# Stick-breaking attention: the diagonal chunks of row blocks 2 and 6 turned by transfers, and the keys copied in place by ScalarE

## The chip, the cores and the metric

The kernel runs on one core of one Trainium2 chip. The metric is the device time of one execution in microseconds (us).

A core has five engines that each follow a queue of their own, in order: PE (TensorE, matrix products; its weight loads are shown apart as PEld), ACT (ScalarE), DVE (VectorE), POOL (GpSimd) and SP (SyncE, which here issues nearly all transfers, DMAs). They meet by semaphores. PE writes to PSUM, an accumulator memory; tiles live in SBUF, 128 partitions wide.

## The reference

A trunk of two layers over 1024 tokens of width 1024: layer 0 has a gated recurrence, layer 1 stick-breaking attention, and each a SwiGLU block behind it. Only the attention is touched by the change. It has 16 heads of width 64:

```python
for blk in range(seq // Q_BLOCK):            # Q_BLOCK = 128
    t0 = blk * Q_BLOCK; t1 = t0 + Q_BLOCK
    z = jnp.einsum("bhqd,bhkd->bhqk", q[:, :, t0:t1], k[:, :, :t1]).astype(jnp.float32) * scale
    strict = s_idx < t_idx                   # causal, the diagonal left out
    log_fail = jnp.where(strict, jax.nn.log_sigmoid(-z), 0.0)
    suffix = lax.cumsum(log_fail, axis=3, reverse=True) - log_fail
    weights = jnp.where(strict, jnp.exp(jax.nn.log_sigmoid(z) + suffix), 0.0)
    outs.append(jnp.einsum("bhqk,bhkd->bhqd", weights.astype(vb.dtype), vb))
```

## The kernel before

**Precision.** Factors are kept as a high and a low part, and products are made from the parts: three matmuls for each product of the dense layers (`mm3`, lines 143 to 145). In attention, a head's queries, 64 wide, stand on one half of the partitions and their low parts on the other half (`Q[q][hx]`). The keys (`KK[q][hx]`, 128 partitions by 2 by 1024) hold the high part in row 0 and the low part in row 1, the same on both halves. So two matmuls over all 128 partitions (`z_part`, L1680 and L1681) give the product of queries and keys.

**Chunks.** For a head, the rows are 8 blocks j of 128 queries. Each block has a diagonal chunk (its keys in the last 512 begun, 128 to 512 wide), and blocks 4 to 7 also a full chunk of 512 keys: 12 chunks a head. A chunk goes through `z_part` (PE), `z_rest` (ACT, a sigmoid, L1693) and `scan` (DVE, a running product from right to left, L1700 and L1703), which leaves the tile `w`.

**Turning.** The products with the values need `w` with keys on the partitions, as two fp16 parts. This is done in two ways:
- `turn_weights`: ACT copies the high part, DVE subtracts the low part (`wx`, L1713 and L1714), and a transposing transfer, issued by SP, writes the turned blocks (`wt` L1721 for full chunks, `wd` L1717 for diagonal ones). Before the change this way is taken by the full chunks and the diagonal chunks of blocks 3 and 7 (`by_transfer`). The four `wx` buffers go round.
- `t_part` and `t_split`: PE turns blocks of 128 by 128 (`wt_ps`, L1732), ACT rounds them to fp16 (`th`, L1741), DVE subtracts (`tl`, L1742). This way is taken by the diagonal chunks of blocks 0, 1, 2 and 4, 5, 6.

`av_part` (L1760) then adds up the products with the values over a *unit*, a block of 128 keys against 512 queries. There are 12 units a head: 4 for the first half of the queries and 8 for the second.

**Order.** Heads come in 8 pairs q, with hx 0 or 1. The queues of PE, ACT, DVE, POOL and SP in attention are written out by hand, in a loop over the 192 units. Each step takes one chunk (10 steps ahead of its unit, 13 ahead near the end), the turning of the chunk before, a unit's products, and 2 parts of the projection of the next pair's queries, keys and values (`qkv_steps`, PE tile `qk_ps`). A pair is thus 24 steps. When the projections run out, at step 161 of 192, the loop has only `out_fill`, parts of the output projection (`ob`); their inputs come back from DRAM by transfers (`back`, L1883).

**Keys.** When a half of a pair's keys is projected, `evacuate` lets DVE scale it into `two`, ACT round the high part (L1663) and DVE subtract the low part (L1645). A step later `spread` has SP issue four transfers (L1642), each of a head's two rows, to the upper and to the lower half of `KK`.

`later` and `soon` are lists of small tasks that the loop takes up one step at a time; a task of `soon` comes at the start of a step.

Of the kernel before, what the change touches and what calls it, by code (L numbers as in the profile page):

```python
# [8 lines left out]
F32 = mybir.dt.float32  # L9
F32R = mybir.dt.float32r  # L10
BF16 = mybir.dt.bfloat16
F16 = mybir.dt.float16
# [5 lines left out]
P = 128  # L18
# [4 lines left out]
NB = 512  # L23
# [11 lines left out]
def trunk(  # L35
# [21 lines left out]
    nc = tc.nc  # L57
    f32 = lambda t: t.bitcast(F32)
# [336 lines left out]
    with ExitStack() as st:  # L395
# [17 lines left out]
        two = lp.tile([P, ND], I32, name="two")  # L413
# [28 lines left out]
        wide = lambda tag, bufs, dt=F32: lp.tile([P, S], dt, tag=tag, name=tag, bufs=bufs)  # L442
# [1045 lines left out]
    with ExitStack() as st:  # L1488
        ap = st.enter_context(tc.tile_pool(name="ap", bufs=1))
# [5 lines left out]
        psQ = qs.enter_context(tc.tile_pool(name="psQ", bufs=2, space=PSUM, side="right", reuse_waits="tile"))  # L1495


        unit = ap.tile([P, NB], F32, name="unit")
        nc.gpsimd.memset(unit[:, 0 : NB - P], 0.0)
        nc.gpsimd.tensor_scalar_mul(unit[:, NB - P :], ident, UP)  # L1500
        g2 = ap.tile([P, ND], BF16, name="g2")
# [2 lines left out]
        Q, KK, VV, VT = {}, {}, {}, {}  # L1504
        top, bot = slice(0, HD), slice(HD, P)
# [14 lines left out]
        def stage(task, steps=1):  # L1520
            soon.append([steps, task])
# [76 lines left out]
        def evacuate(q, which, n, ps):  # L1598
            full = lambda tag, m: [ap.tile([P, m, S], F32R, tag=tag, name=tag, bufs=4 if m == 1 else 3) for _ in range(2)]
            cs = slice(n * NB, (n + 1) * NB)  # L1600
            if which == 2:
                if n == 0:
                    VT[q] = ap.tile([P, S + 1], F32, tag="vt", name="vt", bufs=2)
                    nc.gpsimd.memset(VT[q][:, 0:1], 0.0)
                    VV[q] = ap.tile([P, 2, NT, 2, HD], F16, tag="v", name="v", bufs=2)
                t = ap.tile([P, NB], F32, tag="t", name="t", bufs=1)
                after = VT[q][:, n * NB + 1 : (n + 1) * NB + 1]
                nc.vector.scalar_tensor_tensor(after, ps, f32(sv[q]), rbc[n], op0=ALU.mult, op1=ALU.mult)
                yield
                if q == NP - 1:  # L1610
                    some = [(p, n) for p in range(NP - 2)]
                    bring_back(*some[:3], *([(NP - 2, 0)] * n), *some[3:])
                nc.vector.tensor_sub(t, VT[q][:, cs], after)
                vx = ap.tile([P, 4, 2, P], F16, tag="vx", name="vx", bufs=2)
                t3 = t.rearrange("p (b c) -> p b c", b=4)

                def low():
                    nc.vector.scalar_tensor_tensor(
                        vx[:, :, 1], t3, 1 / UP, vx[:, :, 0], op0=ALU.mult, op1=ALU.subtract
                    )  # L1620
                    for hx, a in enumerate((top, bot)):
                        nc.sync.dma_start(
                            VV[q][:, hx, 4 * n : 4 * n + 4].rearrange("p b h c -> p (b h) c"),
                            vx[a].rearrange("p b h c -> p (b h c)"),
                            transpose=True,
                        )
                def high():
                    nc.scalar.activation(vx[:, :, 0], t3, AF.Copy, scale=1 / UP)
                    stage(low)

                stage(high, 2)
                return
            two = ap.tile([P, 2, NB], F32R, tag="two", name="two", bufs=2)

            def spread():
                for hx, (a, b) in enumerate(((top, bot), (bot, top))):
                    if which == 0:
                        nc.sync.dma_start(f32(Q[q][hx])[a, cs], f32(two)[a, 0])
                        nc.sync.dma_start(f32(Q[q][hx])[b, cs], f32(two)[a, 1])
                    else:  # L1640
                        for half_ in (top, bot):
                            nc.sync.dma_start(f32(KK[q][hx])[half_, :, cs], f32(two)[a])  # L1642

            def low():
                nc.vector.tensor_sub(two[:, 1], t, f32(two)[:, 0])  # L1645
                stage(spread)

            if which == 0:
                t = ps
                if n == 0:  # L1650
                    Q[q] = [x[:, 0] for x in full("q", 1)]
                nc.scalar.copy(two[:, 0], t)
                yield
                low()
            else:
                t = f32(two)[:, 1]
                nc.vector.tensor_mul(t, ps, rbc[n])
                if n == 0:
                    KK[q] = full("kk", 2)
                yield  # L1660

                def high():
                    nc.scalar.copy(two[:, 0], t)  # L1663
                    stage(low)

                stage(high)
# [20 lines left out]

        def z_rest(ps, q, hx, j, ci, c0, c1, diag):
            n = min(c1, (j + 1) * P) - c0
            tag = f"w{j}" if diag and j != 3 else "w"  # L1690
            F = ap.tile([P, n], F32, tag=tag, name=tag, bufs=1 if tag != "w" else 3)
            W[q, hx, j, ci] = F
            nc.scalar.activation(F, ps[:, 0:n], AF.Sigmoid, scale=rs[:, j : j + 1])  # L1693

        def scan(q, hx, j, ci, c0, c1, diag):
            F = W[q, hx, j, ci]
            n = min(c1, (j + 1) * P) - c0
            rev = F[:, ::-1]
            if diag:
# [5 lines left out]
        T = {}  # L1705

        def by_transfer(q, hx, j, ci, c0, c1, diag):
            return not diag or j % 4 == 3

        def turn_weights(q, hx, j, ci, c0, c1, diag):  # L1710
            F = W[q, hx, j, ci].rearrange("p (b c) -> p b c", c=P)
            wx = ap.tile([P, 4, 2, P], F16, tag="wx", name="wx", bufs=4)
            nc.scalar.copy(wx[:, :, 0], F)  # L1713
            nc.vector.tensor_sub(wx[:, :, 1], F, wx[:, :, 0])  # L1714
            if diag:
                T[q, hx, j] = ap.tile([P, 8, P], F16, tag="wd", name="wd", bufs=2)
                nc.sync.dma_start(T[q, hx, j], wx.rearrange("p b h c -> p (b h c)"), transpose=True)  # L1717
                return
            if j == 4:
                T[q, hx] = ap.tile([P, 8, 4, P], F16, tag="wt", name="wt", bufs=2)  # L1720
            nc.sync.dma_start(T[q, hx][:, :, j % 4], wx.rearrange("p b h c -> p (b h c)"), transpose=True)  # L1721

        def unit_list(q, hx):
            kbs = ((0, 1, 2, 3), (4, 5, 6, 7, 0, 1, 2, 3))
# [2 lines left out]
        def t_part(q, hx, G, kb, first, last):  # L1727
            j0 = max(kb, 4 * G)
            tp = psT.tile([P, NB], F32, tag="T", name="wt_ps")
            for j in range(j0, 4 * G + 3):  # L1730
                c = (j - 4 * G) * P
                nc.tensor.transpose(  # L1732
                    tp[:, c : c + P], W[q, hx, j, kb // 4][:, (kb % 4) * P : (kb % 4 + 1) * P], ident
                )
            return tp

        def t_split(tp, q, hx, G, kb, first, last):
            q0 = (max(kb, 4 * G) - 4 * G) * P
            th = ap.tile([P, NB - P], F16, tag="th", name="th", bufs=3)
            tl = ap.tile([P, NB - P], F16, tag="tl", name="tl", bufs=3)  # L1740
            nc.scalar.copy(th[:, q0:], tp[:, q0 : NB - P])  # L1741
            nc.vector.tensor_sub(tl[:, q0:], tp[:, q0 : NB - P], th[:, q0:])  # L1742
            return th, tl

        av, oo = {}, {}
# [1 line left out]
        def av_part(tht, q, hx, G, kb, first, last):  # L1747
            q0 = (max(kb, 4 * G) - 4 * G) * P
            if first:
                av[0] = psO.tile([P, NB], F32, tag="o", name="av_ps")  # L1750
            ps = av[0]
            if kb // 4 != G:
                turned = [T[q, hx][:, 2 * kb + x].rearrange("p j c -> p (j c)") for x in range(2)]
                parts_ = [(0, NB, t, 0) for t in turned]
            else:
                parts_ = [(NB - P, NB, T[q, hx, 4 * G + 3][:, 2 * (kb % 4) + x], 0) for x in range(2)]
                if tht is not None:
                    parts_ = [(q0, NB - P, t, q0) for t in tht] + parts_
            for i, (c0, c1, t, t0) in enumerate(parts_):
                nc.tensor.matmul(  # L1760
                    ps[:, c0:c1], lhsT=VV[q][:, hx, kb], rhs=t[:, t0 : t0 + c1 - c0],
# [4 lines left out]
            a, b = (top, bot)[:: 1 if hx == 0 else -1]  # L1766
# [38 lines left out]
        units = [u for q, hx in heads for u in unit_list(q, hx)]  # L1805
# [28 lines left out]
        with tc.manual_schedule(engines={E.PE, E.Activation, E.DVE, E.Pool, E.SP}):  # L1834
# [33 lines left out]
            c = 0  # L1868
# [5 lines left out]
            for u in range(-LEAD, len(units)):  # L1874
# [9 lines left out]
                for a in some:  # L1884
                    z_rest(z_part(*a), *a)
                    if u % 2 or u < -2:
                        scan(*a)
# [3 lines left out]
                if u % 2 == 0 and u >= 0:  # L1891
                    av_part(ready.pop(u, None), *units[u])
                if u % 2 == 0 and 0 <= u + 2 < len(units):
                    two = {x: t_part(*units[x]) for x in (u + 2, u + 3) if x % 12 < 8 and x % 4 < 3}
                    for x, tp in two.items():
                        ready[x] = t_split(tp, *units[x])
                if u % 2 == 0 and u >= -2:
# [70 lines left out]
```

## Time and profile before

| | |
|---|---|
| time before, median of 3 runs | 2144.06 us (2139.91 to 2144.3) |
| profiled execution | 2142.03 us |
| its span | 2140.0 us |
| granted TensorE clock, mean | 0.997 |
| busy share of the span | PE 99%, DVE 83%, ACT 53%, POOL 6% |
| attention | about 985 to 1420 us of the span |

The profile is of one execution. Its own time is 2.03 us above its span. Busy times are of whole instructions as the profiler has them; matmuls overlap, so a matmul's duration is longer than the time from its start to the next one's start. L numbers are lines of the kernel.

### The profile page before, as it was taken

How to read it: one execution, taken by the hardware profiler on the slowest of the kernel's cores; microseconds unless marked ns; L12 is line 12 of the kernel's file. 1: busy time of each engine (PE TensorE's matmuls, PEld its weight loads, DVE VectorE, ACT ScalarE, POOL GpSimd, SP SyncE). 2: the span in 40 equal slices, each digit the busy share in tenths (PEclk: the TensorE clock that was granted, in tenths of full speed). 3: DMA queues.
4: the chain of work that ended last, by engine and by line, in shares of the span. 5: the costliest groups of instructions: out<-in, count | busy, mean ns of one | idle time of the engine just before them, and what ended most of it. 6: DMA issues, size and time to landing. Idle time of an engine off the chain costs nothing.

```text
span 2140.0 us, 28244 instructions
## 1 busy us (share of the span) xinstructions
PE 2116.5 (99%) x10222; PEld 1735.1 (81%) x10222; DVE 1778.7 (83%) x2609; ACT 1137.5 (53%) x1838; POOL 125.8 (6%) x100
## 2 busy tenths in 40 slices
PE   8999999999999999999999999899999999999998
PEld 7888888888888888888777777678888888888887
DVE  7887768888888888896899999867888888888886
ACT  6567435444443545565666666544544344454556
POOL 1222020000000000000000000002000000000002
PEclk9999999999999999999999999999999999999999
DMA  7111421334445875536888888983234544587442
GB/s 237 50 50 40 153 98 58 117 113 157 138 148 162 276 241 148 160 121 143 160 177 178 176 177 177 230 257 99 64 104 128 162 135 151 193 274 229 130 153 89
DMA packets 424109, 323.87 MB, mean 151 GB/s; under 512 B 135065, under 2 KB 330785, under 8 KB 423969
## 3 DMA queue, kind: packets, MB, share of 16 engines
q1 hardware_dynamic: 423808, 321.80, 53.1%
q8 instruction: 80, 1.31, 0.3%
q14 instruction: 61, 0.49, 0.1%
q10 hardware_dynamic: 160, 0.27, 0.0%
HBM read 184.09 MB, written 83.36 MB: 125 GB/s over the span
## 4 chain that ended last, share of the span: by engine, by line
PE 96%; DVE 2%; DMA 1%; ACT 1%; issue 1%; SPq 0%; DVEq 0%; ACTq 0%
PE p_ps L143 18%; PE p_ps L145 18%; PE p_ps L144 18%; PE qk_ps L143 4%; PE qk_ps L145 4%; PE qk_ps L144 4%; PE av_ps L1760 3%; PE a_ps L144 3%; PE a_ps L145 3%; PE a_ps L143 3%; PE ob_ps L145 3%; PE ob_ps L143 3%; PE ob_ps L144 3%; PE z_ps L1680 2%; PE z_ps L1681 2%; PE i_ps L145 1%
## 5 line engine op out<-in xcount | busy, mean ns | idle before, releaser
L143 PE MATMUL p_ps<-vh,wbh 128*128 128x512 f32 x524 | 204.9, 391 | 0.0
L144 PE MATMUL p_ps<-vl,wbh 128*128 128x512 f32 x524 | 204.5, 390 | 0.0
L145 PE MATMUL p_ps<-vh,wbl 128*128 128x512 f32 x524 | 204.0, 389 | 0.2 <-DVE wbl L726 0.2
L143 PE MATMUL p_ps<-vh,wch 128*128 128x512 f32 x524 | 204.1, 390 | 0.0
L145 PE MATMUL p_ps<-vh,wcl 128*128 128x512 f32 x524 | 204.1, 389 | 0.0
L144 PE MATMUL p_ps<-vl,wch 128*128 128x512 f32 x524 | 203.9, 389 | 0.0
L722 ACT CAST wbh<-sb 128x1024 fp32r<-128x1024 f32 (+2 forms) x69 | 69.6, 1009 | 192.6 <-DVE sb L702 192.6
L1693 ACT ACTIVATE w<-z_ps,rs 128x128 f32<-128x128 f32 (+1 forms) x192 | 110.9, 580 | 94.0 <-PE z_ps L1681 93.5
L145 PE MATMUL p_ps<-vh,wal 128*128 128x512 f32 x396 | 154.0, 389 | 0.0
L143 PE MATMUL p_ps<-vh,wah 128*128 128x512 f32 x396 | 154.0, 389 | 0.0
L144 PE MATMUL p_ps<-vl,wah 128*128 128x512 f32 x396 | 154.0, 389 | 0.0
L145 PEld LDWEIGHTS p_ps<-vh,wbl 128*128 128x128 f32 x524 | 98.4, 188 | 21.6 <-DVE wbl L726 0.7
L145 PEld LDWEIGHTS p_ps<-vh,wcl 128*128 128x128 f32 x524 | 98.3, 188 | 21.0 <-DVE wcl L736 0.6
L144 PEld LDWEIGHTS p_ps<-vl,wch 128*128 128x128 f32 x524 | 98.4, 188 | 20.4
L143 PEld LDWEIGHTS p_ps<-vh,wch 128*128 128x128 f32 x524 | 98.3, 188 | 20.5 <-ACT tb L1181 0.2
L1700 DVE TENSOR_TENSOR_SCAN w<-w,unit 128x128 f32<-128x128 f32 (+3 forms) x128 | 105.0, 831 | 11.7 <-ACT w L1693 11.6
L143 PEld LDWEIGHTS p_ps<-vh,wbh 128*128 128x128 f32 x524 | 98.6, 188 | 19.8 <-ACT U L1181 0.4
L144 PEld LDWEIGHTS p_ps<-vl,wbh 128*128 128x128 f32 x524 | 98.6, 188 | 18.5
L143 PE MATMUL qk_ps<-vh,whi 128*128 128x512 f32 x264 | 111.9, 424 | 0.0
L145 PE MATMUL qk_ps<-vh,wlo 128*128 128x512 f32 x264 | 103.7, 393 | 0.0
L144 PE MATMUL qk_ps<-vl,whi 128*128 128x512 f32 x264 | 103.2, 391 | 0.0
L143 PE MATMUL p_ps<-vh,wd 128*128 128x512 f32 x254 | 99.4, 391 | 0.0
(403 smaller groups left out, 5794.2 us busy)
## 6 DMA issues: line engine op xcount, KB each, us to landing
raw<-in_ffn_w_in SPq DMA_DIRECT2D x88, 512.0 KB, 4.2
vl<-pd SPq DMA_DIRECT2D x128, 256.0 KB, 3.5
pd<-U SPq DMA_DIRECT2D x90, 256.0 KB, 2.3
kk<-two SPq DMA_DIRECT2D x64, 256.0 KB, 4.5
raw<-in_ffn_w_out SPq DMA_DIRECT2D x56, 256.0 KB, 3.7
raw<-in_attn_w_qkv SPq DMA_DIRECT2D x24, 512.0 KB, 5.9
h<-hd SPq DMA_DIRECT2D x32, 256.0 KB, 5.8
hd<-h SPq DMA_DIRECT2D x32, 256.0 KB, 2.0
```

Of the source, the lines that this page charges most:

```text
L143: nc.tensor.matmul(ps, lhsT=wh, rhs=mh, start=first, stop=False, **kw)
L144: nc.tensor.matmul(ps, lhsT=wh, rhs=ml, start=False, stop=False, **kw)
L145: nc.tensor.matmul(ps, lhsT=wl, rhs=mh, start=False, stop=last, **kw)
L722: nc.scalar.copy(self.full(self.wb), self.full(self.sb))
L1680: nc.tensor.matmul(ps[:, 0 : c1 - c0], lhsT=lhsT, rhs=KK[q][hx][:, 0, c0:c1], start=True, stop=False)
L1681: nc.tensor.matmul(ps[:, 0 : c1 - c0], lhsT=lhsT, rhs=KK[q][hx][:, 1, c0:c1], start=False, stop=True)
L1693: nc.scalar.activation(F, ps[:, 0:n], AF.Sigmoid, scale=rs[:, j : j + 1])
L1700: nc.vector.tensor_tensor_scan(rev, rev, unit[:, NB - n :][:, ::-1], 0.0, op0=ALU.mult, op1=ALU.add)
L1760: nc.tensor.matmul(ps[:, c0:c1], lhsT=VV[q][:, hx, kb], rhs=t[:, t0 : t0 + c1 - c0], start=first and i == 0, stop=last and i == len(parts_ ...
```

## The change

Five edits go together.

- Blocks 2 and 6 join those whose diagonal chunk is turned by a transfer (384 wide, so three blocks of high and three of low parts). `wd` holds two row blocks side by side. PE turns only blocks 0, 1, 4 and 5, and `th` and `tl` are 256 wide at most. The products of a unit with the turned diagonal are 256 wide where both row blocks count.
- Keys: a head's half of the partitions gets high and low parts by ScalarE copies within the partitions (four of 64x512 for each half of a pair's keys). Only the high part goes to the other half by a transfer (two of 64x512 for each half of the keys), which is issued one step earlier than before. Beside the low part stand zeros, so the product of the two low parts is left out.
- GpSimd writes these zeros, two of 64x1024 a pair.
- The tile `w` of block 2 comes from the shared three buffers.
- `unit`, the second operand of the diagonal scans, is BF16 instead of F32.

```diff
-        unit = ap.tile([P, NB], F32, name="unit")
+        unit = ap.tile([P, NB], BF16, name="unit")
...
+            sides = ((0, top, bot), (1, bot, top))
+
+            def place(x):
+                for hx, a, b in sides:
+                    if x == 0:
+                        nc.sync.dma_start(f32(KK[q][hx])[b, 0, cs], f32(two)[a, 0])
+                    nc.scalar.copy(KK[q][hx][a, x, cs], f32(two)[a, x])
+
             def spread():
-                for hx, (a, b) in enumerate(((top, bot), (bot, top))):
-                    if which == 0:
-                        nc.sync.dma_start(f32(Q[q][hx])[a, cs], f32(two)[a, 0])
-                        nc.sync.dma_start(f32(Q[q][hx])[b, cs], f32(two)[a, 1])
-                    else:
-                        for half_ in (top, bot):
-                            nc.sync.dma_start(f32(KK[q][hx])[half_, :, cs], f32(two)[a])
+                if which == 1:
+                    place(1)
+                    return
...
             def low():
                 nc.vector.tensor_sub(two[:, 1], t, f32(two)[:, 0])
+                if which == 1:
+                    place(0)
                 stage(spread)
...
                 if n == 0:
                     KK[q] = full("kk", 2)
+                    for hx, a, b in sides:
+                        nc.gpsimd.memset(f32(KK[q][hx])[b, 1], 0.0)
...
-            tag = f"w{j}" if diag and j != 3 else "w"
+            tag = f"w{j}" if diag and j not in (2, 3) else "w"
...
         def by_transfer(q, hx, j, ci, c0, c1, diag):
-            return not diag or j % 4 == 3
+            return not diag or j % 4 >= 2
...
-            for j in range(j0, 4 * G + 3):
+            for j in range(j0, 4 * G + 2):
...
-            nc.scalar.copy(th[:, q0:], tp[:, q0 : NB - P])
-            nc.vector.tensor_sub(tl[:, q0:], tp[:, q0 : NB - P], th[:, q0:])
+            nc.scalar.copy(th[:, q0:], tp[:, q0 : 2 * P])
+            nc.vector.tensor_sub(tl[:, q0:], tp[:, q0 : 2 * P], th[:, q0:])
...
-                parts_ = [(NB - P, NB, T[q, hx, 4 * G + 3][:, 2 * (kb % 4) + x], 0) for x in range(2)]
+                c0 = max(q0, 2 * P)
+                parts_ = [(c0, NB, t, c0 - 2 * P) for t in turned]
...
-                    two = {x: t_part(*units[x]) for x in (u + 2, u + 3) if x % 12 < 8 and x % 4 < 3}
+                    two = {x: t_part(*units[x]) for x in (u + 2, u + 3) if x % 12 < 8 and x % 4 < 2}
```

**PE, at a step that turns blocks for two units.** Before:

```order
L1760 MATMUL av_ps<-wd,v 128x128
L1732 MATMUL wt_ps<-ident,w_8264 128x128
L1732 MATMUL wt_ps<-ident,w_8286 128x128
L1732 MATMUL wt_ps<-ident,w_8303 128x128
L1732 MATMUL wt_ps<-ident,w_8286 128x128
L1732 MATMUL wt_ps<-ident,w_8303 128x128
L143 MATMUL qk_ps<-vh_3_2540,whi 128x512
```

Of the change, at the same step:

```order
L1774 LDWEIGHTS v
L1774 MATMUL av_ps<-wd,v 128x256
L1743 MATMUL wt_ps<-ident,w_8275 128x128
L1743 MATMUL wt_ps<-ident,w_8296 128x128 x2
L143 MATMUL qk_ps<-vh_3_2540,whi 128x512
```

Five turned blocks become three, and the products with the transferred weights are 256 wide. At the next even step one turned block becomes none.

**ACT, where the second half of a pair's keys is placed.** The copies for the keys (`kk`) stand ahead of the sigmoids (`w<-z_ps`) of two steps that follow each other. Before:

```order
L1693 ACTIVATE w<-z_ps,rs 128x512
L1741 CAST th<-wt_ps 128x384
L1741 CAST th<-wt_ps 128x256
L1713 CAST wx<-w_9221 128x4x128
L1693 ACTIVATE w<-z_ps,rs 128x512
L1713 CAST wx<-w 128x4x128
L1558 CAST whi<-raw 128x512
L1693 ACTIVATE w<-z_ps,rs 128x512
L1741 CAST th<-wt_ps 128x128
L1713 CAST wx<-w 128x4x128
L1772 COPY oo<-av_ps 64x512
```

Of the change, at the same steps:

```order
L1704 ACTIVATE w<-z_ps,rs 128x512
L1752 CAST th<-wt_ps 128x256
L1752 CAST th<-wt_ps 128x128
L1725 CAST wx<-w_9205 128x4x128
L1641 CAST kk<-two 64x512 x2
L1704 ACTIVATE w<-z_ps,rs 128x512
L1725 CAST wx<-w 128x4x128
L1558 CAST whi<-raw 128x512
L1641 CAST kk<-two 64x512 x2
L1704 ACTIVATE w<-z_ps,rs 128x512
L1725 CAST wx<-w 128x4x128
L1786 COPY oo<-av_ps 64x512
```

Two copies come ahead of each of two sigmoids; the `th` copies are narrower, and one is gone.

**SP, where the projections run out and the transfers back from DRAM (`odh`, `odl`) begin.** Before:

```order
L1642 DMA kk<-two 64x2x512 x4
L1721 DMA_TRANSPOSE wt<-wx 128x8x128 x2
L1883 DMA vh_3_2532<-odh_0_7885 128x512
L1721 DMA_TRANSPOSE wt<-wx 128x8x128
L1883 DMA vl_3_2533<-odl_0_7886 128x512
L1622 DMA_TRANSPOSE v<-vx 128x8x64 x2
L1883 DMA xg_6477<-odh_0_7887 128x512
L1883 DMA xg_6478<-odl_0_7888 128x512
L1883 DMA vh_3_2540<-odh_0_7889 128x512
L1883 DMA vl_3_2541<-odl_0_7890 128x512
L1883 DMA xg_7655<-odh_0_7891 128x512
L1717 DMA_TRANSPOSE wd<-wx 128x8x128
```

Of the change, the same stretch from the second transfer back on, cut at the same `wd`:

```order
L1732 DMA_TRANSPOSE wt<-wx 128x8x128
L1897 DMA vl_3_2533<-odl_0_7886 128x512
L116 DMA raw<-in_attn_w_o 128x8x128
L1622 DMA_TRANSPOSE v<-vx 128x8x64 x2
L1897 DMA xg_6477<-odh_0_7887 128x512
L1897 DMA xg_6478<-odl_0_7888 128x512
L1897 DMA vh_3_2540<-odh_0_7889 128x512
L1732 DMA_TRANSPOSE wd<-wx 128x6x128
L1897 DMA vl_3_2541<-odl_0_7890 128x512
L1897 DMA xg_7655<-odh_0_7891 128x512
L1732 DMA_TRANSPOSE wd<-wx 128x8x128
```

A transposing transfer for block 2 has come in, and a load of output weights (512 KB) that stood some 35 rows further on now stands ahead of the values' transfers.

More of the change, by code (lines that the diff above doesn't have):

```diff
@@ L1633, in evacuate @@
             two = ap.tile([P, 2, NB], F32R, tag="two", name="two", bufs=2)
-            def spread():
-                for hx, (a, b) in enumerate(((top, bot), (bot, top))):
-                    if which == 0:
-                        nc.sync.dma_start(f32(Q[q][hx])[a, cs], f32(two)[a, 0])
-                        nc.sync.dma_start(f32(Q[q][hx])[b, cs], f32(two)[a, 1])
-                    else:
-                        for half_ in (top, bot):
-                            nc.sync.dma_start(f32(KK[q][hx])[half_, :, cs], f32(two)[a])
+            sides = ((0, top, bot), (1, bot, top))
[4 more added lines that the diff above has]
+                    nc.scalar.copy(KK[q][hx][a, x, cs], f32(two)[a, x])
+            def spread():
+                if which == 1:
+                    place(1)
+                    return
+                for hx, a, b in sides:
+                    nc.sync.dma_start(f32(Q[q][hx])[a, cs], f32(two)[a, 0])
+                    nc.sync.dma_start(f32(Q[q][hx])[b, cs], f32(two)[a, 1])
             def low():
                 nc.vector.tensor_sub(two[:, 1], t, f32(two)[:, 0])
+                if which == 1:
+                    place(0)
                 stage(spread)
@@ L1659, in evacuate @@
                     KK[q] = full("kk", 2)
+                    for hx, a, b in sides:
+                        nc.gpsimd.memset(f32(KK[q][hx])[b, 1], 0.0)
                 yield
@@ L1707, in by_transfer @@
         def by_transfer(q, hx, j, ci, c0, c1, diag):
-            return not diag or j % 4 == 3
+            return not diag or j % 4 >= 2
         def turn_weights(q, hx, j, ci, c0, c1, diag):
             F = W[q, hx, j, ci].rearrange("p (b c) -> p b c", c=P)
+            m = F.shape[1]
             wx = ap.tile([P, 4, 2, P], F16, tag="wx", name="wx", bufs=4)
[L1713 to L1721, printed above, removed]
+            nc.scalar.copy(wx[:, 0:m, 0], F)
+            nc.vector.tensor_sub(wx[:, 0:m, 1], F, wx[:, 0:m, 0])
+            g = (q, hx, j // 4, diag)
+            if g not in T:
+                wide, tag = (2, "wd") if diag else (4, "wt")
+                T[g] = ap.tile([P, 8, wide, P], F16, tag=tag, name=tag, bufs=2)
+            dst = T[g][:, 0 : 2 * m, j % 4 - (2 if diag else 0)]
+            nc.sync.dma_start(dst, wx[:, 0:m].rearrange("p b h c -> p (b h c)"), transpose=True)
         def unit_list(q, hx):
@@ L1738, in t_split @@
             q0 = (max(kb, 4 * G) - 4 * G) * P
[L1739 to L1742, printed above, removed]
+            th = ap.tile([P, 2 * P], F16, tag="th", name="th", bufs=3)
+            tl = ap.tile([P, 2 * P], F16, tag="tl", name="tl", bufs=3)
+            nc.scalar.copy(th[:, q0:], tp[:, q0 : 2 * P])
+            nc.vector.tensor_sub(tl[:, q0:], tp[:, q0 : 2 * P], th[:, q0:])
             return th, tl
@@ L1751, in av_part @@
             ps = av[0]
+            turned = [
+                T[q, hx, G, kb // 4 == G][:, 2 * (kb % 4) + x].rearrange("p j c -> p (j c)") for x in range(2)
+            ]
             if kb // 4 != G:
-                turned = [T[q, hx][:, 2 * kb + x].rearrange("p j c -> p (j c)") for x in range(2)]
                 parts_ = [(0, NB, t, 0) for t in turned]
             else:
-                parts_ = [(NB - P, NB, T[q, hx, 4 * G + 3][:, 2 * (kb % 4) + x], 0) for x in range(2)]
+                c0 = max(q0, 2 * P)
+                parts_ = [(c0, NB, t, c0 - 2 * P) for t in turned]
                 if tht is not None:
-                    parts_ = [(q0, NB - P, t, q0) for t in tht] + parts_
+                    parts_ = [(q0, 2 * P, t, q0) for t in tht] + parts_
             for i, (c0, c1, t, t0) in enumerate(parts_):
```

## Prediction

> **What bounds the kernel now.** I read the page first, for the busy shares.
>
> ```profile
> PE 2116.5 (99%) x10222; PEld 1735.1 (81%) x10222; DVE 1778.7 (83%) x2609; ACT 1137.5 (53%) x1838; POOL 125.8 (6%) x100
> ```
>
> The span is PE's, but a share is a mean over stages. So next come the busy times by stretch, cut at the start of PE's turned blocks, which makes each stretch one head. Columns: stretch, length, then busy time (and instructions) of PE, PEld, DVE, ACT and POOL, the granted clock, the DMA share, GB/s.
>
> ```profile
> 1108.79:1135.47 26.68, 26.68 (x146) 20.33 (x145) 24.24 (x35) 17.70 (x35) 1.09 (x1) 1.00 0.84 185
> 1135.47:1162.45 26.98, 26.98 (x155) 20.62 (x153) 25.38 (x40) 17.55 (x35) 2.80 (x4) 1.00 0.93 170
> ...
> 1350.11:1376.00 25.89, 22.99 (x123) 16.74 (x121) 24.42 (x39) 16.61 (x33) 1.71 (x3) 0.88 0.98 202
> ```
>
> PE fills two heads (a pair, 53.66 us) without a gap. DVE has 49.62 of these 53.66 us, so 4.04 us of room. From about 1366 us, where the projections end, PE has gaps. PE's waits between 985 and 1425 us, as total, times, longest, show where:
>
> ```profile
> PE ob L143 <- DMA vh<-odh: 4.2, 3, 1.7
> PE z_ps L1680 <- ACT w L1693: 2.5, 3, 1.9
> PE ob L144 <- DMA vl<-odl: 1.4, 3, 1.0
> ```
>
> All three belong to the end, waits for what comes back from DRAM and for sigmoids. So there are two stages: 14 heads bound by PE, and an end of some 50 us that is not. Windows of 10 us of the end:
>
> ```profile
> 1360.00:1370.00 10.00, 8.06 (x49) 6.15 (x47) 9.94 (x17) 5.36 (x12) 0.00 (x0) 1.00 1.09 204
> 1370.00:1380.00 10.00, 7.97 (x21) 4.57 (x21) 9.42 (x13) 5.47 (x9) 0.00 (x0) 0.66 0.95 216
> 1380.00:1390.00 10.00, 7.09 (x37) 4.55 (x37) 7.14 (x12) 5.24 (x12) 0.00 (x0) 1.00 1.14 302
> 1390.00:1400.00 10.00, 7.35 (x47) 4.58 (x44) 9.01 (x14) 6.67 (x14) 0.00 (x0) 0.86 1.08 284
> ```
>
> Here the DMA engines are full, and DVE has 35.5 of 40 us: those two share the bound.
>
> **PE's part.** What PE's instructions cost in flow is read from the chain of waits, which merges neighbours (start, length, count):
>
> ```profile
> 1140.43 0.45 PE av_ps L1760 x4
> ...
> 1144.23 0.34 PE av_ps L1760 x4
> ...
> 1144.86 0.24 PE av_ps L1760 x4
> 1145.10 0.55 PE wt_ps L1732 x5
> ```
>
> A turned block costs 0.55/5 = 0.11 us. A group of four blocks of queries had 3 + 2 + 1 turned blocks and now has 2 + 1: 0.33 us less, 0.66 us a head. The products: the three av rows are units of columns 2 x (384 + 128), 2 x (256 + 128) and 2 x (128 + 128). They are now 2 x (256 + 256), 2 x (128 + 256) and 2 x 256: the same columns, in fewer pieces in the third. At 0.45 us for 1024 columns this is nothing. So 14 heads x 0.66 = **9.2 us less** on the bounding engine; 1.3 us more in the last two heads, which I count at nothing since PE waits there anyway (bound: 1.3 gained).
>
> **What takes PE's place: DVE and ACT.** The groups by shape between 1000 and 1400 us (busy us, mean ns | idle before):
>
> ```profile
> L1714 DVE TENSOR_TENSOR wx<-w,wx 128x512 f16<-128x512 f32 x90 | 64.4, 716 | 7.3 <-ACT wx L1713 6.4
> L1713 ACT CAST wx<-w 128x512 f16<-128x512 f32 x91 | 56.7, 624 | 30.1 <-DVE w L1700 12.9 <-DVE w L1703 9.1 <-DMA wd<-wx 2.9
> L1700 DVE TENSOR_TENSOR_SCAN w<-w,unit 128x512 f32<-128x512 f32 x31 | 39.8, 1284 | 7.2 <-ACT w L1693 7.2
> ...
> L1772 ACT COPY oo<-av_ps 64x512 f32<-64x512 f32 x29 | 16.9, 582 | 0.7
> L1742 DVE TENSOR_TENSOR tl<-wt_ps,th 128x384 f16<-128x384 f32 x30 | 16.5, 551 | 14.2 <-ACT th L1741 14.2
> L1741 ACT CAST th<-wt_ps 128x384 f16<-128x384 f32 x30 | 14.4, 480 | 3.9 <-PE wt_ps L1732 2.6
> ...
> L1742 DVE TENSOR_TENSOR tl<-wt_ps,th 128x256 f16<-128x256 f32 x30 | 12.4, 412 | 0.0
> ...
> L1645 DVE TENSOR_TENSOR two<-two 128x512 fp32r<-128x512 f32 x14 | 9.5, 680 | 0.0
> ```
>
> Widths 384, 256, 128 become 256, 128, none: what goes is one 384 wide, 0.551 us on DVE and 0.480 on ACT a group. What comes is one `wx` pair 384 wide. At three quarters of the 512 rows this is 0.54 on DVE and 0.47 on ACT. The sum is zero on both. It moves, though, from the steps where DVE is fullest (full chunks, scans of 512) to those of the diagonal.
>
> The keys' ScalarE copies are new: 8 a pair, at the 0.582 us of the only 64x512 copy (L1772, out of PSUM), 4.7 us a pair. ACT has 35.2 of 53.66 us, so there is room, but they stand ahead of sigmoids for which DVE waits. The tightest place, the second half of a pair's keys:
>
> ```profile
> 1139.19 0.68 DVE L1645 TENSOR_TENSOR two<-two 128x512 fp32r<-128x512 f32 x1
> ...
> 1140.47 0.69 ACT L1693 ACTIVATE w<-z_ps,rs 128x512 f32<-128x512 f32 x1 [0.21 <-PE z_ps L1681]
> 1141.20 0.63 ACT L1713 CAST wx<-w 128x512 f16<-128x512 f32 x1
> 1141.86 0.69 DVE L1714 TENSOR_TENSOR wx<-w,wx 128x512 f16<-128x512 f32 x1
> ...
> 1147.89 0.88 DVE L1742 TENSOR_TENSOR tl<-wt_ps,th 128x384 f16<-128x384 f32 x2
> 1149.01 0.34 PE L1760 MATMUL av_ps<-th,v 128*128 128x384 f16 x1
> ```
>
> The first `tl` is done at 1147.89 + 0.55 = 1148.44. PE wants it for its second product, half of a 0.34 us pair after 1149.01, at 1149.18: 0.74 us of slack. PE will come 2 + 1 + 2 turned blocks earlier, 0.55 us. The low parts' copies wait for DVE's subtraction, done at 1139.87, and two last 1.16, to 1141.03. The sigmoid then ends at 1141.7 instead of 1141.16, the `wx` copy at 1142.3 instead of 1141.83, and DVE's subtraction comes 0.5 us late; the whole queue of DVE shifts, as it is full there. The narrower `tl` gives back 0.14 (551 to 412). So 0.74 - 0.55 - 0.5 + 0.14 = -0.17: PE waits 0.17 us in each of the 7 pairs whose keys are placed inside the loop, **1.2 us back**. Bounds: nothing (ACT is ahead), and the pair's whole gain, 1.3 us, 9 us in all.
>
> In the other head of a pair no keys are placed; by the same sum the slack stays over 0.2 us.
>
> `unit` in BF16: no row shows a scan with it. A subtraction with an fp16 side lasts 716 against 680 ns (L1714, L1645), so the bounds are none and 5% of 1.28 us a scan, either way; DVE has the room, so I take nothing.
>
> **POOL's zeros.** Rows of POOL: start, length.
>
> ```profile
> 965.32 0.42 POOL L1499 MEMSET unit<- 128x384 f32 x1 [642.58 <-DVE rbc L1383]
> ...
> 1153.34 1.09 POOL L1777 TENSOR_TENSOR oo<-oo,vt 128x512 f32<-128x512 f32 x1 [12.12 <-DVE oo L1773]
> 1171.24 2.12 POOL L1777 TENSOR_TENSOR oo<-oo,vt 128x512 f32<-128x512 f32 x1 [16.82 <-DVE oo L1773]
> ```
>
> Scaled by width, a memset of 1024 lasts 0.42 x 1024/384 = 1.1 us, 2.2 a pair, queued ahead of POOL's small factors only, with POOL idle for 12 us and more at a time. The same addition lasts 1.09 or 2.12 us, so POOL and DVE do hold each other up. I take nothing; the bound is that DVE stands still for all 2.2 us. The Trainium skill (SBUF — State Buffer, "Who interferes with whom") says that a VectorE instruction with two SBUF inputs contends with a GpSimd one that reads SBUF, not with one that only writes: by it the zeros cost DVE nothing, and no row here shows a large memset beside such an instruction.
>
> **Transfers.** Rows of SP's issues and one of landing (us at the end):
>
> ```profile
> 1030.87 1.27 SPq L1717 DMA_TRANSPOSE wd<-wx  x1
> ...
> 1035.68 3.41 SPq L1642 DMA_DIRECT2D kk<-two  x4
> ...
> 1047.33 0.58 SPq L116 DMA_DIRECT2D raw<-in_attn_w_qkv  x1
> ...
> 1055.49 0.51 SPq L1638 DMA_DIRECT2D q<-two  x1
> ...
> wd<-wx SPq DMA_TRANSPOSE x30, 3.6
> ```
>
> A pair loses 8 transfers of 256 KB and gains 4 of 128 KB and 4 transposing ones of 192 KB. SP: -6.8 + 4 x 0.55 + 4 x 1.27 = +0.5 us. Bytes: -0.75 MB; a turned byte costs the engines more than a copied one, so I call the load equal. The new transposing transfers are issued a step after their chunk and needed 7 steps later (a step is 53.66/24 = 2.24 us, so 15.7 us), against 3.6 us to landing: hidden. The Trainium skill (VectorE: DVE Perf Modes, "The three transpose paths") speaks against this edit: 1309 ns for a 128x128 block by a transfer against 390 on TensorE. By it, as an estimate, a 384 wide transfer of both parts takes 6 x 1.31 = 7.9 us; the row, 3.6 us for eight blocks, is far below, and decides.
>
> At the end SP and the DMA engines are full. There SP loses one set of keys (3.41 to about 1.1), and gains four transposing issues (4 x 1.27) and, ahead of the values, a weight load of 0.58 that stood later: +3.4 us. As DVE has the other half of this bound, I take a third, **1.2 us**. Bounds: -1.3 (PE's blocks count after all), and 3.4 + 1.7 (the load's 512 KB at 302 GB/s) = 5.1.
>
> **The sum.** -9.2 + 1.2 + 1.2 = -6.8 us. The profiled execution took 2142.03 (span 2140.0 and 2.03 around it), which makes 2135.2; from the median of 2144.06 it is 2137.3. I take 2136. A measurement of this kernel can tell some 0.2% (4.3 us) from no change.
>
> **Rivals.**
> 1. *ACT and DVE become the bound, slower.* Place: the steps where keys are placed. If DVE keeps all its idle time (4.04 us a pair, waits on ACT) and half of the 4.7 us of key copies falls in front of its scans, a pair lasts 53.66 + 2.3 us, and 7 pairs 16 us more: 2158. It decides from 2.7 us of DVE idle time a pair (4.04 less PE's 1.3). For it: DVE at 94% in one head, L1713's 30 us of idle time ahead. Against: ACT's 66%, and that the waits on ACT come where DVE has caught up. 0.15.
> 2. *The gain is eaten at the handoff*: DVE just keeps up with the old pace, 0 in place of -9.2, and the end's 1.2: 2143. POOL holding DVE for 2.2 us a pair would come to this too. 0.17.
> 3. *The end takes it back*: -9.2 + 1.2 + 5.1 = -2.9, 2139, within 0.2%. For it the DMA shares over 1, against it DVE's 9.9 and 9.4. 0.10.
> 4. *The change doesn't do what it says.* The order of instructions shows the narrower turning and half as many key transfers, so I give it nothing.
>
> Forecast: 0.55. Something slower that I don't see: 0.03.
>
> **Range and chances.** The forecast's best is 9.2 + 1.3 + 1.3 below the profiled time, 2130. Above, rivals 2 and 3 reach 2143, the median's side 2145, and DVE's part of rival 1 in small 2149. The range 2130 to 2149 leaves out most of rival 1 and the unseen. Faster by over 0.2% is the forecast, less 0.03 of it that ends close: 0.52. Within 0.2%: 0.03 + 0.17 + 0.10 = 0.30. Slower: 0.18.
>
> **What would show it.** Right: a pair of 52.5 us with PE full, DVE near 49.6 in it, and PE's wait for `tl` of some 0.2 us a pair; the end from the last projection to the last product 1 us longer. Wrong: a pair at 53.66 or more, with PE waiting for `tl` or for sigmoids (rivals 1 and 2), DVE rows stretched beside memsets (the zeros), or waits of `ob` for `vh` and `vl` well over 6 us (rival 3).

## The result, and the profile after

| | before | after |
|---|---|---|
| median of 8 runs each | 2143.78 us (2139.91 to 2144.72) | 2137.22 us (2135.17 to 2138.37) |
| profiled execution | 2142.03 | 2137.39 |
| its span | 2140.0 | 2135.6 |

The ratio is 0.9972, with a 95% interval of 0.9963 to 0.9981: 6.6 us faster by the medians. The forecast was 2136, so 1.2 us from it.

The page's busy times of after, in the order of those of before:

```profile
PE 2106.9 (99%) x10062; PEld 1725.7 (81%) x10062; DVE 1776.9 (83%) x2609; ACT 1173.4 (55%) x1902; POOL 142.6 (7%) x116
```

PE has 160 instructions and 9.6 us of busy time less, ACT 36 us more, and DVE is where it was. The windows of after, cut as before: two heads of one pair, then 10 us pieces of the end (length, busy time of PE, PEld, DVE, ACT, POOL, granted clock, DMA share, GB/s).

```profile
1107.18:1133.07 25.89, 25.89 (x136) 19.70 (x135) 24.76 (x37) 20.19 (x39) 4.03 (x3) 1.00 0.95 199
1133.07:1159.51 26.44, 26.33 (x144) 19.96 (x143) 24.58 (x39) 19.65 (x39) 2.73 (x4) 1.00 0.69 135
...
1360.00:1370.00 10.00, 6.73 (x24) 3.88 (x24) 9.94 (x16) 5.98 (x12) 0.00 (x0) 0.86 1.16 272
1370.00:1380.00 10.00, 5.87 (x22) 3.63 (x23) 6.03 (x9) 3.32 (x8) 0.00 (x0) 0.84 1.07 228
1380.00:1390.00 10.00, 9.15 (x41) 5.99 (x39) 7.54 (x12) 4.73 (x11) 0.00 (x0) 0.62 1.08 266
```

The pair is 25.89 + 26.44 = 52.33 us, against 53.66: the heads are still PE's. PE's waits from 985 to 1425 us (total, times, longest):

```profile
PE z_ps L1691 <- ACT w L1704: 6.4, 6, 2.5
PE ob L143 <- DMA vh<-odh: 4.1, 1, 4.1
PE av_ps L1774 <- DVE oo L1787: 0.9, 1, 0.9
PE ob L144 <- DMA xg<-odl: 0.8, 1, 0.8
PE av_ps L1774 <- DVE tl L1753: 0.8, 2, 0.7
PE av_ps L1774 <- DMA wt<-wx: 0.7, 2, 0.3
```

The first two belong to the end. The wait for sigmoids has grown from 2.5 to 6.4 us; those for `vh` are 4.1 us in all, as before (4.2), but in one piece. Last comes a small new wait inside the heads, for the transfers of the full chunks (`wt`), in two of the pairs. The handoff's wait for `tl`, 0.27 us in most pairs, hardly shows in this list, as the recorded length of the matmul ahead covers most of it; it is read from starts, below. Here is the end, from the last projection to the last run of products, as one window; of before, after, and of a version with the last pair turned as before (e3 below):

```profile
1365.37:1418.35 52.98, 42.63 (x215) 28.28 (x214) 43.65 (x63) 28.07 (x55) 2.89 (x2) 0.90 1.05 260
```

```profile
1358.35:1413.65 55.30, 42.72 (x193) 27.26 (x191) 43.96 (x63) 27.97 (x56) 2.87 (x2) 0.88 1.09 256
```

```profile
1358.68:1412.66 53.98, 44.42 (x213) 29.95 (x212) 43.92 (x63) 28.09 (x56) 2.87 (x2) 0.84 1.01 257
```

The end is 2.3 us longer in the profiled execution, at a DMA share (last column but one) of 1.09 in the mean. Length times share is 55.6 us before, 60.3 after, 54.5 in e3.

### The profile page after: what moved, and what is told of

The parts are those of the page before. It is cut to its first block, busy times and chain, and to the rows that moved or that the text cites. A ratio compares the mean times of both kernels' runs of the same rounds, so it can differ in the third digit from the quotient of the medians.

```text
span 2135.6 us, 28098 instructions
## 1 busy us (share of the span) xinstructions
PE 2106.9 (99%) x10062; PEld 1725.7 (81%) x10062; DVE 1776.9 (83%) x2609; ACT 1173.4 (55%) x1902; POOL 142.6 (7%) x116
## 4 chain that ended last, share of the span: by engine, by line
PE 89%; DVE 5%; issue 2%; ACT 2%; DMA 1%; SPq 0%; DVEq 0%; ACTq 0%
PE p_ps L143 18%; PE p_ps L145 18%; PE p_ps L144 18%; PE a_ps L144 3%; PE a_ps L145 3%; PE a_ps L143 3%; PE ob_ps L144 3%; PE ob_ps L145 3%; PE ob_ps L143 3%; PE qk_ps L143 2%; PE qk_ps L144 2%; PE qk_ps L145 2%; PE av_ps L1774 2%; PE i_ps L145 1%; PE i_ps L144 1%
## 5 line engine op out<-in xcount | busy, mean ns | idle before, releaser
L1725 ACT CAST wx<-w 128x512 f16<-128x512 f32 (+1 forms) x128 | 75.9, 593 | 57.1 <-DVE w L1711 21.1
```

The costliest lines, as they stand in the source:

```text
L1725: nc.scalar.copy(wx[:, 0:m, 0], F)
```

## The experiments

Theory H is that of the prediction: PE's blocks are the gain, ACT's copies of the keys cost a wait for `tl` once a pair, the end costs a little. Its rivals: the keys' part helps by relieving transfers; the gain is in something other than the turned blocks; the zeros hold DVE. The pair is taken from one traced execution, between the same instruction of successive pairs without a wait for `wt`. The end is from the last projection to the last product. Two versions that hardly differ there, after and e8, have ends 1.6 us apart, so a smaller difference of one end says nothing.

| | median, us | ratio to before (95%) | pair, us | end, us |
|---|---|---|---|---|
| before | 2142.64 and 2143.14 | | 53.66 | 52.98 |
| after | 2137.22 | 0.9972 (0.9963 to 0.9981) | 52.33 | 55.30 |
| e1, turning alone | 2136.42 | 0.9970 (0.9960 to 0.9981) | 52.06 | 56.93 |
| e2, keys alone | 2144.88 | 1.0011 (1.0002 to 1.0020) | 53.92 | 52.23 |
| e3, last pair as before | 2135.23 | 0.9964 (0.9952 to 0.9977) | 52.33 | 53.98 |
| e4, blocks given back to PE | 2141.80 | 0.9995 (0.9986 to 1.0004) | 53.42 | 54.42 |
| e5, key copies twice | 2175.59 | 1.0150 (1.0136 to 1.0164) | 58.05 | |
| e6, key copies later | 2133.18 | 0.9955 (0.9943 to 0.9968) | 52.06 | 54.43 |
| e7, e6 with e3 | 2132.46 | 0.9953 (0.9939 to 0.9966) | 52.06 | 52.52 |
| e8, zeros three times | 2136.73 | 0.9970 (0.9959 to 0.9982) | 52.33 | 53.68 |

The runs of before are 8 beside after (2143.78, above), 23 beside e1 to e4 and 10 beside e5 to e8; each ratio is to those beside it.

### e1: the turning alone, keys as before

```diff
             def spread():
                 if which == 1:
-                    place(1)
+                    for hx, a, b in sides:
+                        for half_ in (top, bot):
+                            nc.sync.dma_start(f32(KK[q][hx])[half_, :, cs], f32(two)[a])
                     return
...
-                if which == 1:
-                    place(0)
...
-                    for hx, a, b in sides:
-                        nc.gpsimd.memset(f32(KK[q][hx])[b, 1], 0.0)
```

> The wider transfers of the weights alone; the keys go by four transfers of 256 KB per half again. Theory P (PE's turned blocks bound a pair of heads, and the keys' part only makes room): a pair falls towards 52.4 us, but the DMA engines, 0.885 busy over a pair before, now get four transposing transfers more and lose nothing, some 1.0; so part of the gain goes, and the end grows: 2138 to 2143. Theory D (the gain is the keys' lighter transfers): no gain, 2144 or more.

The pair is 52.06 us: the whole of PE's gain, 1.60 us, with no handoff wait. The total is that of after, and below the expected 2138 to 2143; in the traced execution its end is 1.6 us longer, about what its pairs save. What the keys' part does for the transfers shows in windows of five pairs (1060 to 1330 us; before, after, e1; the DMA share is the last but one column):

```profile
1060.00:1330.00 270.00, 270.00 (x1491) 206.17 (x1490) 249.60 (x374) 177.74 (x344) 22.59 (x25) 1.00 0.88 176
```

```profile
1060.00:1330.00 270.00, 268.80 (x1422) 204.38 (x1421) 253.74 (x379) 204.85 (x392) 36.21 (x38) 1.00 0.80 165
```

```profile
1060.00:1330.00 270.00, 269.03 (x1429) 205.19 (x1428) 256.18 (x382) 182.47 (x353) 22.61 (x26) 1.00 1.00 195
```

The transposing transfers add 0.12 to the DMA engines' share and the keys take 0.20 away. At a share of 1.00 late `wt` transfers lengthen two of e1's pairs, by 0.3 and 1.0 us; at 0.80 two of after's, by 0.5 each. So in the heads the relief is worth little. Why those pairs were hit stays open.

### e2: the keys alone, turning as before

```diff
             def spread():
-                for hx, (a, b) in enumerate(((top, bot), (bot, top))):
...
-                        for half_ in (top, bot):
-                            nc.sync.dma_start(f32(KK[q][hx])[half_, :, cs], f32(two)[a])
+                if which == 1:
+                    place(1)
+                    return
...
+                if which == 1:
+                    place(0)
...
+                    for hx, a, b in sides:
+                        nc.gpsimd.memset(f32(KK[q][hx])[b, 1], 0.0)
```

> The keys' copies and zeros alone; blocks 2 and 6 are turned by PE as before. Theory P: a pair stays at 53.66 us, and only the end can gain the 2 us of issues that SP loses: 2141 to 2144. Theory D: most of the 6.6 us gained, 2137 to 2139. Theory A (ScalarE's copies cost what DVE then lacks): over 2144, with waits of PE for sigmoids or tl.

Slower, by 2.2 us of medians; the interval's lower end is just above 1. That is what was expected under theory A. The pair grows by 0.26 us, and this lies at one place, PE's rows of the first `tl` of the pair:

```profile
1151.18 0.34 PE L1771 MATMUL av_ps<-th,v 128*128 128x384 f16 x1
1151.62 0.32 PE L1771 MATMUL av_ps<-tl,v 128*128 128x384 f16 x1
```

Between the two starts lie 0.44 us; in the units of this width where no keys are placed, and in before at this place (1149.01 and 1149.18), 0.17 or 0.18. So the copies cost the handoff even when PE comes no earlier.

### e3: the last pair's blocks 2 and 6 turned by PE as before

```diff
+        own = lambda q: 3 if q == NP - 1 else 2
...
-            return not diag or j % 4 >= 2
+            return not diag or j % 4 >= own(q)
...
-            for j in range(j0, 4 * G + 2):
+            for j in range(j0, 4 * G + own(q)):
```

The wider `th` and `tl` of this pair, and its `w` of block 2, stand in a buffer for keys that is free by then.

> The change, but in the last pair of heads blocks 2 and 6 are turned by PE as before, so that the end has four transposing transfers less. Theory P: the end is bound by transfers and the four wx buffers, and loses the 2 us that it grew by: 2134.5 to 2136. If the end is bound by DVE or PE instead: 2137 to 2138.5.

The median is 2.0 us below that of after (other runs of before beside it: 7.4 us below them, against 6.6). The ratios' intervals overlap, so the times don't decide it. The traced end does point that way: 54.5 us of DMA work (length times share, above) in place of 60.3, and an end 1.3 us shorter. So does the table as a whole: the ends with the last pair turned by transfers (after, e1, e4, e6, e8) are 53.7 to 56.9 us long, 55.0 in the mean, those with PE turning it (before, e2, e3, e7) 52.2 to 54.0, 52.9 in the mean.

### e4: twelve turned blocks a pair given back to PE

```diff
+            for x in range(2 - kb % 4):
+                nc.tensor.transpose(
+                    tp[:, (2 + x) * P : (3 + x) * P], W[q, hx, 4 * G + 1, G][:, (kb % 4) * P : (kb % 4 + 1) * P], ident
+                )
             return tp
```

The extra blocks go to columns that nobody reads; they are as many as the change took from PE.

> The change, with three turned blocks more for each group on PE, written to unused columns: as many as before the change, 96 in all. Theory P: 14 heads x 0.66 us come back, 2145.5 to 2147, and a pair lasts 53.66 us again. If transfers, DVE or ACT set a pair's time by now, PE has room for them: 2137 to 2140.

Nearly all of the gain is gone: 0.9995, no difference from before. The time is under the expected 2145.5 to 2147, since waits of after go as the blocks come back. PE's rows at the handoff of e4:

```profile
1150.64 0.28 PE L1778 MATMUL av_ps<-th,v 128*128 128x256 f16 x1
1150.76 0.27 PE L1778 MATMUL av_ps<-tl,v 128*128 128x256 f16 x1
```

The starts are 0.12 us apart, no wait: PE comes so much later that `tl` is there. Its pair is to be held against one that doesn't wait either (e1, e6): 53.42 - 52.06 = 1.36 us for 12 blocks, 0.113 us each.

### e5: each key copy twice

```diff
-                    nc.scalar.copy(KK[q][hx][a, x, cs], f32(two)[a, x])
+                    for _ in range(2):
+                        nc.scalar.copy(KK[q][hx][a, x, cs], f32(two)[a, x])
```

> The change, with each ScalarE copy of the keys made twice (the suspected cost doubled: 8 more copies of 0.62 us a pair). Theory H (handoff: the copies delay a sigmoid, then wx, then DVE, and PE waits for the first tl of the unit group once a pair, 0.27 us in the change): two more copies, 1.25 us, stand ahead of each of the two sigmoids, so PE waits some 1 to 1.3 us more there; a pair lasts 53.3 to 53.7 us, and the time is 2143 to 2147. If ScalarE has room (its busy share in attention is about 75%), 2136 to 2138 and a pair of 52.35.

The direction is that of H, the size far off: 38 us slower than after, 5.7 us a pair. ACT has room in the mean (44.03 of 58.00 us in a pair), yet at the step DVE stands still for 2.84 us for `wx` from ACT (it was 1.01 in after, below). PE's waits over five pairs (1060 to 1330 us), and three windows of 2 us, at the end of one of the long waits and behind it:

```profile
PE av_ps L1775 <- DVE tl L1754: 8.9, 4, 2.3
PE z_ps L1692 <- ACT w L1705: 2.5, 4, 0.6
PE n_ps L1537 <- ACT sq L1553: 2.0, 4, 0.5
```

```profile
1162.00:1164.00 2.00, 0.94 (x5) 0.82 (x5) 2.00 (x6) 1.30 (x3) 0.00 (x0) 0.84 0.67 130
1164.00:1166.00 2.00, 2.00 (x7) 1.51 (x6) 2.00 (x5) 0.75 (x2) 0.00 (x0) 0.50 0.54 104
1166.00:1168.00 2.00, 2.00 (x9) 1.55 (x7) 1.94 (x3) 0.94 (x2) 0.42 (x1) 0.80 0.57 93
```

The three waits are 13.4 us over four pairs, 3.3 a pair, and behind the wait for `tl` the granted clock falls to half. What the clock falls short of 1 in the three windows is (0.16 + 0.50 + 0.20) x 2 us = 1.7 us; with the waits that is 5.0 of the 5.7, and the rest was not placed. At the handoff 2.5 us of added copies (two ahead of each of two sigmoids) make the wait for `tl` 2.2 us and that for a sigmoid 0.6, so its slack is used up in after, and what comes on top goes to PE.

### e6: the second half of the keys placed later

```diff
+                if which == 1 and n == 1:
+                    stage(lambda: place(0), 3)
+                    stage(spread, 4)
+                    return
                 if which == 1:
                     place(0)
```

> The change, with the second half of a pair's keys placed three steps later, behind the steps that have the full chunks. Theory H: PE's wait of 0.27 us goes, a pair lasts 52.06 us as with the weights' transfers alone, 2 us less over seven pairs: 2134 to 2135.5. If the 0.27 us is another cost of the copies or zeros (contention, more waits in PE's queue): no change, 2136 to 2137.5.

PE's rows of the same place in e6:

```profile
1145.49 0.28 PE L1778 MATMUL av_ps<-th,v 128*128 128x256 f16 x1
1145.61 0.27 PE L1778 MATMUL av_ps<-tl,v 128*128 128x256 f16 x1
```

No wait, and a pair of 52.06 us, that of e1. The copies themselves are free here; what costs is their place ahead of the sigmoid. (Two transfers of the keys move with them; their share was not tested apart.) Against before in the same batch it is 10.0 us faster. The median is 4.0 us below that of after, more than the 2 us expected: the handoff makes 2.4 of it by the traces, and `wt` came late once, by 0.24 us, in place of twice.

### e7: e6 with the last pair turned as in e3

The edits of both.

> Both: the keys' second half placed three steps later, and the last pair turned by PE as before the change. If the two costs are separate, the gains add: 1.9 us in the seven pairs and 1 to 2 us in the end, 2132 to 2134. If the end's time does not depend on when it starts (it is bound by transfers that wait on nothing before it): only one of them, 2134 to 2136.

The fastest of all: 0.9953 (0.9939 to 0.9966), faster than before, and than the change as it was made with intervals that overlap by 0.0003. Over e6 it gains 0.7 us of medians, which these runs can't tell from nothing; its traced end is 1.9 us shorter.

### e8: the zeros written three times

```diff
-                        nc.gpsimd.memset(f32(KK[q][hx])[b, 1], 0.0)
+                        for _ in range(3):
+                            nc.gpsimd.memset(f32(KK[q][hx])[b, 1], 0.0)
```

> The change, with GpSimd's zeros written three times (4 memsets of 0.95 us more a pair). If a memset that only writes does not hold VectorE up: the change's time, 2136 to 2138, a pair of 52.35, and VectorE's rows beside memsets as long as elsewhere. If they do: VectorE loses up to 3.8 us a pair and has about 1.5 left, so a pair lasts up to 2 us longer, 2140 to 2150.

POOL is busy 17 us more in 270, and neither the pair nor DVE moves (253.90 us here, 253.74 in after):

```profile
1060.00:1330.00 270.00, 268.46 (x1422) 204.00 (x1421) 253.90 (x379) 203.90 (x391) 52.83 (x59) 1.00 0.80 165
```

## Why the prediction was right, step by step

**PE's blocks: right, and a little small.** 0.66 us a head was predicted, 1.32 a pair; without the handoff the pair lost 1.60. A block costs 0.113 us by e4, as the 0.11 of the chain said, so the blocks are 1.36. The rest, 0.24 a pair, is where "the same columns" was counted at nothing. PE's timeline in one group of blocks, before and after (start, length):

```profile
1140.27 0.34 PE L1760 MATMUL av_ps<-th,v 128*128 128x384 f16 x1
...
1140.76 0.47 PE L143 MATMUL qk_ps<-vh,whi 128*128 128x512 f32 x1
...
1144.07 0.28 PE L1760 MATMUL av_ps<-th,v 128*128 128x256 f16 x1
...
1144.38 0.36 PE L1680 MATMUL z_ps<-kk,q 128*128 128x256 f32 x1
...
1144.70 0.23 PE L1760 MATMUL av_ps<-th,v 128*128 128x128 f16 x1
...
1144.93 0.71 PE L1732 MATMUL wt_ps<-ident,w 128*128 128x128 f32 x5
1145.40 0.47 PE L143 MATMUL qk_ps<-vh,whi 128*128 128x512 f32 x1
```

```profile
1137.83 0.29 PE L1774 MATMUL av_ps<-th,v 128*128 128x256 f16 x1
...
1138.20 0.48 PE L143 MATMUL qk_ps<-vh,whi 128*128 128x512 f32 x1
...
1141.52 0.23 PE L1774 MATMUL av_ps<-th,v 128*128 128x128 f16 x1
...
1141.78 0.36 PE L1691 MATMUL z_ps<-kk,q 128*128 128x256 f32 x1
...
1142.10 0.39 PE L1774 MATMUL av_ps<-wd,v 128*128 128x256 f16 x2
...
1142.32 0.49 PE L1743 MATMUL wt_ps<-ident,w 128*128 128x128 f32 x3
1142.57 0.48 PE L143 MATMUL qk_ps<-vh,whi 128*128 128x512 f32 x1
```

From start to start: the first unit with its lone block 0.49 and 0.37; the second unit 0.31 and 0.26; the third 0.23 and 0.22; the turned blocks 0.47 and 0.25. The differences are 0.12 + 0.05 + 0.01 + 0.22 = 0.40 a group, four groups a pair: 1.60. One block less in the first difference and two in the last are 0.34; the second and third units make the other 0.06. The rows show that these are products; why they are shorter at the same columns stays open.

**The handoff: right in its place and size, by two errors that cancel.** Predicted was 0.17 us a pair at the first `tl`; it is 0.27. The rows of after, DVE, ACT and PE:

```profile
1136.62 0.68 DVE L1652 TENSOR_TENSOR two<-two 128x512 fp32r<-128x512 f32 x1
1140.10 0.69 DVE L1726 TENSOR_TENSOR wx<-w,wx 128x512 f16<-128x512 f32 x1 [1.01 <-ACT wx L1725]
1146.12 0.61 DVE L1753 TENSOR_TENSOR tl<-wt_ps,th 128x256 f16<-128x256 f32 x2
```

```profile
1137.07 0.61 ACT L1558 CAST whi<-raw 128x512 fp32r<-128x512 f32 x1
1137.59 1.25 ACT L1641 CAST kk<-two 64x512 fp32r<-64x512 f32 x2
1138.87 0.69 ACT L1704 ACTIVATE w<-z_ps,rs 128x512 f32<-128x512 f32 x1
```

```profile
1146.19 0.28 PE L1774 MATMUL av_ps<-th,v 128*128 128x256 f16 x1
1146.58 0.27 PE L1774 MATMUL av_ps<-tl,v 128*128 128x256 f16 x1
```

The prediction let the copies begin when DVE's subtraction ends. ACT had a cast of the weights (`whi`) ahead of them then, and the pair of copies lasts 1.25, not 1.16. So from the subtraction to `wx` DVE takes 3.48 us (1136.62 to 1140.10) in place of 2.67 (1139.19 to 1141.86): 0.81 late, not 0.5, though the lone block's `tl` of some 0.3 us no longer stands between. On the other side PE comes only 0.25 us earlier against DVE's subtraction (9.82 us from 1139.19 to 1149.01 before, 9.57 now), not 0.55: two of the five blocks lie ahead of that subtraction. And PE now wants `tl` 0.12 us after `th`, not 0.17. With the prediction's 0.74 and 0.14 the sum is 0.74 - 0.25 - 0.81 + 0.14 - 0.05 = -0.23, near the 0.27 seen. In the first pair the wait is 0.82 us. e6 shows the cause: with the copies elsewhere the wait is gone.

**ACT and DVE (rival 1): rightly set low, but nearer than it looked.** DVE's work in a pair is 49.34 us (25.89 and 26.44 us long heads, 24.76 + 24.58), against 49.62: the sums of zero held. A key copy lasts 618 ns in place of the 582 predicted, and the scan with a BF16 `unit` 1278 in place of 1284, so that edit is worth nothing. Groups by shape of after (1000 to 1400 us):

```profile
L1711 DVE TENSOR_TENSOR_SCAN w<-w,unit 128x512 f32<-128x512 f32 x31 | 39.6, 1278 | 0.4 <-ACT w L1704 0.3
...
L1641 ACT CAST kk<-two 64x512 fp32r<-64x512 f32 x56 | 34.6, 618 | 1.0
```

Rival 1's price was 2.3 us a pair for half of the copies falling ahead of scans. With them doubled, e5 shows 5.7. It is no lack of DVE's time (49.59 of 58.00 us in a pair of e5) but the waits on ACT at the steps where keys are placed, as the rival had it, and after stands at its threshold.

**POOL's zeros: right.** Nothing, by e8. The rule that the Trainium skill states (SBUF — State Buffer, "Who interferes with whom"), that GpSimd's writes do not hold a VectorE instruction with two SBUF inputs, agrees with it: 17 us more of them, 0.2 us of DVE.

**The transfers: the step "I call the load equal" was wrong, though no cost of it shows.** The share fell from 0.88 to 0.80; of that the turned chunks are +0.12 and the keys -0.20 (e1). The new transfers are hidden as forecast; DMA issues of after (median us to landing; with the 384 wide ones among them):

```profile
wd<-wx SPq DMA_TRANSPOSE x55, 3.4
```

A small term was missing: the full chunks' transfers came late in two pairs, which lasted 52.80 and 52.81 us, 0.9 us in all, at a share below that of before.

**The end: the sign right, the size unsure.** Predicted +1.2 with bounds of -1.3 and 5.1; the traced one is +2.3, and e8's, of the same program there, +0.7. PE's waits for what comes back from DRAM (4.1 us for `vh`, 0.8 for `xg`) stay under the 6 us that were to speak for rival 3; what grew is the wait for sigmoids, which the prediction's sum of SP's issues did not have. ACT's longest wait in the end, for a `wx` tile that a `wd` transfer still reads, is 4.4 us in after, 2.9 in before and in e3. That the last pair's transposing transfers are part of the longer end is supported by this, by e3's DMA work and by the ends in the table, but not shown by the times.

**Sum.** Seven pairs: -11.2 for PE, +1.9 for the handoff and 0.55 more in the first pair, +0.9 for `wt`, +2.3 for the end, and 0.6 us by which attention began later: -4.95, where the traced executions differ by -4.6. The other 0.3 us were not placed. The medians differ by -6.6, the forecast was -6.8. So the mechanism was right, but that the total came this close is luck in part: against the prediction's terms PE gained 2.0 us more, handoff, end, `wt` and the later start took 3.9 us more back, and the medians differ by 2.0 us more than the two traced executions. The lower end of the range counts the 1.3 us of the last two heads twice, as PE's and as the end's: by its own terms it should be 2131.5.

## What to carry to other kernels

A copy on an engine that is half idle is free only where nothing is queued behind it that the bounding engine needs soon: list the whole queue at that step, casts of weights too, and place the copy a step or two later if its reader allows. When the bound engine is relieved, each handoff has that much less slack, so look for the tightest one and count only the work that lies between the two instructions. A doubled cost tells how near a threshold is, which the share of busy time does not.

## What the runs showed of the hardware

In e5 a wait of PE of 2.25 us was followed by a granted clock of 0.50 in the window 1164 to 1166 us, with 0.80 in the next. In after the end has a granted clock of 0.72 from 1365 to 1370 us, behind a wait of 2.5 us that ended at 1366.06, and of 0.62 from 1380 to 1390 us, behind the wait of 4.1 us. The Trainium skill (TensorE: Matmul & The Clock Gate, "Part 1: The HAM clock gate (the "warmup" mystery)") puts the fall after an idle window of about 3.4 us; here the clock also fell behind waits of 2.25 and 2.5 us, so a wait of some 2 us on the bounding engine can cost more than its length, in e5 some 1.7 us more.
